# Retention in token-major form: all values and gates by seven products of halves, and the last dense layer's norm factor applied per token

## The chip, the cores and the metric

One core of a Trainium2 chip runs the whole program. The time is device microseconds from launch to end; lower is better. The kernel before was run three times: 1354.38, 1354.49 and 1355.02 us, median 1354.49. One further execution was recorded by the hardware profiler; its span is 1353.1 us.

Engines are called by the profile's names: PE is TensorE (PEld its weight loads), DVE VectorE, ACT ScalarE, POOL GpSimd, and SP the engine that issues most DMA transfers.

## What is computed

A trunk of two residual layers over 512 tokens of width 1024. Layer 0 mixes by a chunked spatial gating MLP, layer 1 by retention; each is followed by a dense MLP with a squared ReLU. Cut to what matters here:

```python
def retention(xn, w_in, head_norm_g, w_out):
    q, k, v, g = split(xn @ w_in)          # 4 heads: q, k of 256, v, g of 512
    q, k = rotary(q, cos, sin), rotary(k * dk ** -0.5, cos, sin)
    ...                                    # causal scores with decay; o = scores @ v
    o = rmsnorm(o, head_norm_g)            # per head
    return (o * silu(g)) @ w_out

def squared_relu_mlp(h, w1, w2):
    a = relu(h @ w1)
    return (a * a) @ w2

for i in range(2):
    x = x + mixer_i(rmsnorm(x, norm_mix_g[i]))
    x = x + squared_relu_mlp(rmsnorm(x, norm_ffn_g[i]), mlp_w1[i], mlp_w2[i])
return rmsnorm(x, final_norm_g)
```

## The kernel before

**Precision.** Every operand of a large matmul is split in two: a rounded high part (ACT copies, L234 for weights) and the difference (DVE subtracts, L241). A product is three matmuls: high x high, high x low, low x high (`mm3`, L277 to L281). A 128-wide piece over the whole width of 1024 is 24 matmuls.

**Tiling.** Tokens lie along the moving side in the feature-major stages: a tile holds 128 features by 512 tokens. The residual `xT` is kept so. In the token-major stages a tile holds 128 tokens by 512 features.

**Steps and pieces.** The program is a list of steps. Each takes weight pieces of 128 x 1024 numbers. After the matmuls of a step, `refill` puts in the splitting of the pieces to come: the high part three pieces ahead, the low part two ahead. Between steps hang hooks ("behind" a step), and `advance` moves unfinished chains of evacuations one stage on. So each engine's order is fixed in the code; what an engine reaches late delays all that stands behind it on that engine. Weights come in transfers of 1 MB into two buffers of their own (`raw`), and in some stretches also into spare large buffers (`more`).

**Seven products of halves.** `seven` (L480) computes a 1024 x 1024 block for 512 tokens as Strassen does: the tokens, the contraction and the output are each halved, and seven products of halves take the place of eight, 24 matmuls each, 168 instead of 192. Sums of weight halves are made by the DMA itself: an accumulating transfer, issued by POOL, adds one half onto another. Sums of activation halves ("sides": `sa`, `sd`, `sp`) are made by DVE and ACT and split in high and low. The products land in PSUM in token-major form and are added to the output tile by DVE; the first addition to a tile is a copy by ACT. Products are numbered 0 to 6; a `form` call makes the side of one of them.

**Retention before.** Values of heads 0 and 1 come by seven products (`smva`, `smvb`, `smvc`), interleaved with q/k pieces of head 0 and gate pieces of head 0. Values of heads 2 and 3 (`vv`) come by plain token-major products, all gates (`g`) by plain feature-major pieces. Attention (`av`, L1143) works on chunks of 128 features: for each of four key blocks it multiplies the values by the scores of all later tokens, so its matmuls are 512, 384, 256 and 128 columns wide. The norm of a head needs a sum over features, which lie along partitions: squares are summed by POOL, two matmuls with ones (`st_h`) add across partitions, and a third (`bc_h`) spreads the factor to all partitions. DVE multiplies it in and splits (`make_y`).

**The dense layers.** `dense` runs up pieces (feature-major) and seven products (token-major) in turn. In both layers an up piece is evacuated by DVE (ReLU and the norm factor, L953) and squared by ACT (L954).

## Time and profile before

| | |
|---|---|
| median of three runs | 1354.49 us |
| span of the profiled execution | 1353.1 us |
| DVE busy | 868.0 us |
| ACT busy | 581.0 us |
| mixer of layer 1 (retention) on PE | 619.0 to 1013.2 us |
| last dense layer on PE | 1013.2 to 1344.7 us |
| bytes moved by DMA | 182.43 MB |

How to read the rows: a timeline row gives the start in us from the span's start, the duration, the engine, the line, the operation, and output <- inputs by the program's names; "x4" merges four in a row, and brackets hold the idle time before it and what ended it. A group row ends with "| busy us, mean ns | idle before". A row of windows gives the stretch, its length, busy time (and count) of PE, PEld, DVE, ACT and POOL, the granted PE clock, the DMA share and GB/s.

### The profile page before, as it was taken

Reading aid. Unit: us, or ns where it says so; the run is one execution under the profiler, and the core shown is the slowest. Engines: PE = TensorE matmul, PEld = TensorE weight load, DVE = VectorE, ACT = ScalarE, POOL = GpSimd, SP = SyncE. Lnnn points to the kernel's source line nnn. Section 1 sums busy time; section 2 is a strip of 40 time slices with the busy share of each in tenths; the row PEclk is TensorE's granted clock in tenths of the full one; section 3 lists DMA queues with packets and bytes.
Section 4 is the critical chain, followed back from the end, with each engine's and each line's share of the span. In section 5 each row is a group of like instructions: output and inputs, shape, how many; then the busy total and the mean of one; then the engine's idle time right before and its main releaser. Section 6 shows DMA issues by size and latency. Waiting matters only on the chain.

```text
span 1353.1 us, 15298 instructions
## 1 busy us (share of the span) xinstructions
PE 1342.5 (99%) x6106; PEld 1117.2 (83%) x6106; DVE 868.0 (64%) x1101; ACT 581.0 (43%) x827; POOL 190.3 (14%) x145
## 2 busy tenths in 40 slices
PE   9999999999999999999999999999999999999997
PEld 7888888888888888888888888888888888888886
DVE  7754456665656656678946456557494675665697
ACT  5655443235544434524533343224333543443464
POOL 4100121130100000012201101111221000100003
PEclk9999999999999999999999999999999999999999
DMA  8662221245674747515712122221126375686763
GB/s 304 169 166 81 90 94 63 93 151 152 149 203 127 215 129 182 167 61 191 172 63 93 63 90 91 85 93 64 63 94 201 106 182 140 169 202 172 198 171 94
DMA packets 124439, 182.43 MB, mean 135 GB/s; under 512 B 3200, under 2 KB 68304, under 8 KB 124368
## 3 DMA queue, kind: packets, MB, share of 16 engines
q1 hardware_dynamic: 105040, 143.17, 31.2%
q0 software_dynamic: 19008, 37.75, 16.2%
q8 instruction: 48, 0.79, 0.2%
q10 hardware_dynamic: 320, 0.53, 0.1%
q14 instruction: 23, 0.19, 0.0%
HBM read 179.35 MB, written 2.10 MB: 134 GB/s over the span
## 4 chain that ended last, share of the span: by engine, by line
PE 97%; DVE 2%; ACT 1%; POOL 0%; issue 0%; ACTq 0%; POOLq 0%; DVEq 0%
PE up L281 24%; PE qk L281 6%; PE u L281 6%; PE o L281 6%; PE g L281 6%; PE ro L281 6%; PE dn L281 2%; PE vv L281 2%; PE av L281 2%; PE v L852 2%; PE smva L281 2%; PE smwa L281 2%; PE v L281 2%; PE sm12a L281 2%; PE sm11a L281 2%; PE sm10a L281 2%
## 5 line engine op out<-in xcount | busy, mean ns | idle before, releaser
L241 DVE TENSOR_TENSOR wL<-raw,wH 128x1024 fp32r<-128x1024 f32 x235 | 305.0, 1301 | 43.8 <-ACT wH L234 15.6
L234 ACT CAST wH<-raw 128x1024 fp32r<-128x1024 f32 x235 | 245.3, 1045 | 63.5 <-ACT wH L234 8.9
L281 PE MATMUL up<-hH,wH 128*128 128x512 f32 x480 | 187.2, 390 | 0.2 <-ACT xtok L1283 0.2
L281 PE MATMUL up<-hH,wL 128*128 128x512 f32 x480 | 186.8, 389 | 0.0
L281 PE MATMUL up<-hL,wH 128*128 128x512 f32 x480 | 186.8, 389 | 0.0
L953 DVE SCALAR_TENSOR_TENSOR r<-up,wide 128x512 f32<-128x512 f32 x54 | 37.4, 692 | 153.6 <-PE up L281 146.2
L954 ACT ACTIVATE aF<-r 128x512 f32<-128x512 f32 x54 | 34.2, 633 | 222.6 <-DVE r L953 222.6
L281 PEld LDWEIGHTS up<-hH,wH 128*128 128x128 f32 x480 | 90.1, 188 | 18.9 <-ACT xtok L1283 0.5
L281 PEld LDWEIGHTS up<-hH,wL 128*128 128x128 f32 x480 | 90.1, 188 | 18.9
L281 PEld LDWEIGHTS up<-hL,wH 128*128 128x128 f32 x480 | 90.1, 188 | 18.7
L207 POOL DMA_DIRECT2D raw<-in_mlp_w_dram x25 | 33.1, 1381 | 437.9 <-DVE wL L241 193.1
L310 POOL TENSOR_TENSOR ssq<-ssq,sq 128x512 f32<-128x512 f32 x28 | 44.1, 1577 | 117.0 <-ACT sq L309 116.7
L241 DVE TENSOR_TENSOR wL<-more,wH 128x1024 fp32r<-128x1024 f32 x42 | 51.0, 1217 | 4.5 <-issue 3.0
L234 ACT CAST wH<-more 128x1024 fp32r<-128x1024 f32 x42 | 44.0, 1047 | 15.9 <-ACT wH L234 6.0
L281 PE MATMUL o<-yH,wH 128*128 128x512 f32 x128 | 50.8, 396 | 0.0
L281 PE MATMUL g<-hH,wH 128*128 128x512 f32 x128 | 50.5, 394 | 0.0
L281 PE MATMUL u<-hH,wH 128*128 128x512 f32 x128 | 50.2, 393 | 0.0
L281 PE MATMUL qk<-hH,wH 128*128 128x512 f32 x128 | 50.0, 391 | 0.0
L281 PE MATMUL ro<-ryH,wH 128*128 128x512 f32 x128 | 49.9, 390 | 0.0
L281 PE MATMUL u<-hH,wL 128*128 128x512 f32 x128 | 49.9, 390 | 0.0
L281 PE MATMUL ro<-ryH,wL 128*128 128x512 f32 x128 | 49.9, 390 | 0.0
L281 PE MATMUL g<-hH,wL 128*128 128x512 f32 x128 | 49.9, 390 | 0.0
(450 smaller groups left out, 3050.1 us busy)
## 6 DMA issues: line engine op xcount, KB each, us to landing
raw<-in_mlp_w_dram SPq DMA_DIRECT2D x50, 1024.0 KB, 5.1
raw<-in_mlp_w_dram POOLq DMA_DIRECT2D x25, 1024.0 KB, 8.8
raw<-in_b_w_in_dram SPq DMA_DIRECT2D x22, 1024.0 KB, 5.0
more<-in_mlp_w_dram SPq DMA_DIRECT2D x21, 1024.0 KB, 5.3
raw<-in_a_w_in_dram SPq DMA_DIRECT2D x10, 1024.0 KB, 5.3
raw<-in_a_w_out_dram SPq DMA_DIRECT2D x8, 1024.0 KB, 4.9
raw<-in_b_w_out_dram SPq DMA_DIRECT2D x8, 1024.0 KB, 4.8
morew<-in_a_w_in_dram SPq DMA_DIRECT2D x5, 1024.0 KB, 8.5
```

What stands on the lines that cost most here:

```text
L207: nc.gpsimd.dma_start(out=r.tile, in_=src, accum_op=ALU.add)
L234: nc.scalar.copy(out=p.hi, in_=p.src)
L241: nc.vector.tensor_sub(out=p.lo, in0=p.src, in1=f32(p.hi))
L281: nc.tensor.matmul(ps, lhsT=a, rhs=b, start=start and i == 0, stop=stop and i == 2, skip_group_check=resumed)
L310: nc.gpsimd.tensor_tensor(out=state["ssq"], in0=state["ssq"], in1=sq, op=ALU.add)
L852: nc.tensor.matmul(accs0[n], lhsT=h[kk][:, n * P : (n + 1) * P], rhs=w, start=kk == 0 and j == 0, stop=kk == 7 and j == 2)
L953: nc.vector.scalar_tensor_tensor(out=r, in0=ps, scalar=0.0, in1=rbc, op0=ALU.max, op1=ALU.mult)
L954: nc.scalar.activation(a, r, AF.Square)
```

## The change

1. All values and all gates of retention come by seven products of halves: four runs of two heads each (`v` and `g` for heads 0 and 1, `w` and `j` for heads 2 and 3). The values run and the gates run of a pair share their sides (`kept`). For the second pair the sides are made from hF, the sum of the high and low parts of the normed input (`side_f`, `whole`), since the residual has been added to by then. The gates runs take the products in the order 1, 4, 0, 3, 5, 2, 6.
2. Attention and gating are token-major: `av` makes 128 tokens by 512 features at a time from the key blocks up to that token block. The head's norm is a sum along the free axis that ACT makes with the square; the gated output is multiplied by it per token and then transposed by PE (`turned`), which ACT and DVE evacuate as the high and low part.
3. The rotary tables take the place of the norm factor's tile, and decay tables are loaded head by head.
4. In the last dense layer the norm factor is left out of the up pieces. ReLU and square are both done by ACT; since the factor enters squared, its square (a power of -1 instead of -0.5) is applied per token where the products are added (`scaled`).

The core of the diff:

```diff
+    def norm_squares(name):
+        yield from stats(state["ssq"], r2s[:, 0, :], 1.0 / D, name, mone)
+        nc.vector.tensor_scalar(out=r2s[:, 1, :], in0=r2s[:, 0, :], scalar1=-1.0, scalar2=0.0, op0=ALU.mult, op1=ALU.add)
...
+        def add_to(m, n, t, op, bank):
+            m, n = 2 * m + t, 1 - n if swap else n
+            v, sign = dst[n][:, m, :], op == ALU.subtract
+            if (n, m // 2) in fresh:
+                nc.scalar.activation(v, bank, AF.Copy, scale=-1.0 if sign else 1.0)
+            elif scaled:
+                nc.vector.scalar_tensor_tensor(out=v, in0=bank, scalar=r2s[:, int(sign), m : m + 1], in1=v, op0=ALU.mult, op1=ALU.add)
+            else:
+                nc.vector.tensor_tensor(out=v, in0=v, in1=bank, op=op)
...
+            if l == 1:
+                nc.scalar.activation(a, ps, AF.Relu)
+                nc.scalar.activation(a, a, AF.Square)
+                return iter(())
...
+        def whole(b):
+            aF[8 + b] = hF[b] = big([P, 4, T], F32, f"hF{b}")
+            for i in range(4):
+                nc.vector.tensor_add(out=hF[b][:, i, :], in0=f32(hH[4 * b + i]), in1=f32(hL[4 * b + i]))
...
-    def av(h, c):
+    def av(h, n):
...
-        for j in range(NT):
-            s = slice(POFF[j], POFF[j] + T - j * P)
-            mm3(ps[:, j * P :], vhi[:, j, cs], vlo[:, j, cs], ph[:, s], pl[:, s], j == 0, j == NT - 1)
+        for j in range(n + 1):
+            s = slice(POFF[j] + (n - j) * P, POFF[j] + (n - j + 1) * P)
+            mm3(ps, ph[:, s], pl[:, s], vhi[:, j, :], vlo[:, j, :], j == 0, j == n)
...
+            y, ss, ms, r = gates(h)[:, n, :], ssh[:, h, n : n + 1], msh[:, h, n : n + 1], rh[:, h, n : n + 1]
+            nc.vector.tensor_tensor(out=y, in0=ps, in1=y, op=ALU.mult)
+            nc.scalar.activation(tmp(f"sqh{h}{n}", "sq"), ps, AF.Square, accum_out=ss)
+            yield
+            nc.vector.tensor_scalar(out=ms, in0=ss, scalar1=1.0 / DV, scalar2=EPS, op0=ALU.mult, op1=ALU.add)
+            rsqrt(r, ms, 1)
+            nc.scalar.activation(y, y, AF.Copy, scale=r)
...
+    def turned(h, c, bank=acc):
...
+            nc.tensor.transpose(ps[:, n * P : (n + 1) * P], gates(h)[:, n, c * P : (c + 1) * P], ident)
...
+        nc.scalar.activation(hi, ps, AF.Copy, scale=g)
+        nc.vector.scalar_tensor_tensor(out=lo, in0=ps, scalar=g, in1=f32(hi), op0=ALU.mult, op1=ALU.subtract)
...
+    hooksV[0].update({(0, 0): nxt(nrm1), (1, 0): norm_ready, (3, 0): lambda: form_v[0](5)})
+    take("vqqvqvqvvvv", v=prodV[0], q=qk_pieces(0, {0: nxt(nrm1, 2), 3: lambda: form_v[0](4)}))
...
+    take("gggqgqgqgqg", g=prodG[0], q=qk_pieces(1, {}, (acc, acc)))
...
+    hooksV[1].update({(0, 0): some(turned, 1, (0, 1)), (0, 1): some(turned, 1, (2, 3))})
+    take("vovovoovvvv", v=prodV[1], o=o_pieces(1))
...
+    take("gggqgqgqqgg", g=prodG[1], q=qk_pieces(3, {2: lambda: silu(2, range(4)), 3: some(av, 2, (0, 1))}, (acc, acc)))
+    do(lambda: (some(turned, 2, range(4))(), split_v(3, range(4)), silu(3, range(4))))
+    take("oooo", o=o_pieces(2, {0: some(av, 3, (0, 1)), 1: some(av, 3, (2, 3)), (3, 0): some(turned, 3, range(4))}))
+    take("oooo", o=o_pieces(3, {}, FFN + 8))
```

In the strings of `take`, v and g are products (two pieces, 24 matmuls), q is a q/k piece and o an output piece (24 matmuls each).

How the order of instructions moves is shown at three places. First DVE in the first values run, from the low part of product 3's last weights on. Names: wL is the low part of a weight piece, sav and spv the sums and the split side of the next product, m the rotary products of q/k, qkL their low part. In the kernel before, wL_4849 belongs to a gate piece and wL_4876 and wL_4905 to product 4:

```order
L241 TENSOR_TENSOR wL_4818<-raw_4105,wH_4817 128x1024
L1080 TENSOR_TENSOR m_4853<-qk_4741,tab 128x512
L1081 TENSOR_TENSOR m_4856<-qk_4741,tab 128x512
L1082 TENSOR_TENSOR m_4854<-qk_4823,tab 128x512
L1083 TENSOR_TENSOR m_4855<-qk_4823,tab 128x512
L241 TENSOR_TENSOR wL_4849<-raw_4684,wH_4848 128x1024
L618 SCALAR_TENSOR_TENSOR sav<-xT_87,gT,sav 128x256 x4
L648 TENSOR_TENSOR spv_4879<-sav,spv_4879 128x512 x2
L1092 TENSOR_TENSOR qkL_4688<-m_4853,qkH_4687 128x512
L1092 TENSOR_TENSOR qkL_4688<-m_4855,qkH_4687 128x512
L241 TENSOR_TENSOR wL_4876<-morev_4544,wH_4875 128x1024
L241 TENSOR_TENSOR wL_4905<-morev_4544,wH_4904 128x1024
```

In the changed kernel, after the same wL (wL_4821), the same engine has these; wL_4852 and wL_4891 are the two halves of product 4's weights:

```order
L638 SCALAR_TENSOR_TENSOR sav<-xT_92,gT,sav 128x256 x4
L668 TENSOR_TENSOR spv_4859<-sav,spv_4859 128x512 x2
L1155 TENSOR_TENSOR m_4868<-qk_4743,wide 128x512
L1156 TENSOR_TENSOR m_4871<-qk_4743,wide 128x512
L1157 TENSOR_TENSOR m_4869<-qk_4826,wide 128x512
L1158 TENSOR_TENSOR m_4870<-qk_4826,wide 128x512
L250 TENSOR_TENSOR wL_4852<-raw_4772,wH_4851 128x1024
L638 SCALAR_TENSOR_TENSOR sav<-xT_91,gT,sav 128x256 x4
L668 TENSOR_TENSOR spv_4894<-sav,spv_4894 128x512 x2
L1167 TENSOR_TENSOR qkL_4687<-m_4868,qkH_4686 128x512
L1167 TENSOR_TENSOR qkL_4687<-m_4870,qkH_4686 128x512
L250 TENSOR_TENSOR wL_4891<-raw_4772,wH_4890 128x1024
```

The gate piece's wL is gone, side 4 has moved ahead of the rotary products, and side 5 (the second sav and spv) now stands between the two halves of product 4's weights.

Second, DVE where a head's output is made ready for its output pieces. Before (head 1; gt is the gated output, ryL its low part, ro the output pieces' results), this lies among head 0's output pieces:

```order
L785 TENSOR_TENSOR xT_87<-xT_87,ro_20_6074 128x512
L241 TENSOR_TENSOR wL_6068<-raw_5967,wH_6067 128x1024
L1184 TENSOR_TENSOR gt_5411<-gt_5411,wide 128x512 x2
L1187 TENSOR_TENSOR ryL_6109<-gt_5411,ryH_6108 128x512 x2
L785 TENSOR_TENSOR xT_87<-xT_87,ro_21_6091 128x512
L785 TENSOR_TENSOR xT_87<-xT_87,ro_30_6117 128x512
L241 TENSOR_TENSOR wL_6105<-raw_5967,wH_6104 128x1024
```

In the changed kernel ryL comes from the transposes (yt) that PE makes between and behind the halves of product 0 of the second values run; hF is the recombined input, sax and spx the side of product 1, and wL_5998 the low part of the first output piece of head 1:

```order
L1103 TENSOR_TENSOR hF_6003<-hH_4415,hL_4416 128x512 x4
L805 TENSOR_TENSOR xT_92<-xT_92,ro_31_5981 128x512
L250 TENSOR_TENSOR wL_5998<-raw_5895,wH_5997 128x1024
L597 TENSOR_TENSOR sax_6028<-hF_5961,hF_6003 128x512
L597 TENSOR_TENSOR sax_6031<-hF_5961,hF_6003 128x512
L616 TENSOR_TENSOR spx_6027<-sax_6028,spx_6027 128x512
L616 TENSOR_TENSOR spx_6027<-sax_6031,spx_6027 128x512
L1236 SCALAR_TENSOR_TENSOR ryL_6037<-yt_6038,gT,ryH_6036 128x512
L1236 SCALAR_TENSOR_TENSOR ryL_6037<-yt_6045,gT,ryH_6036 128x512
L250 TENSOR_TENSOR wL_6024<-raw_5886,wH_6023 128x1024
L1236 SCALAR_TENSOR_TENSOR ryL_6037<-yt_6068,gT,ryH_6036 128x512
L1236 SCALAR_TENSOR_TENSOR ryL_6037<-yt_6075,gT,ryH_6036 128x512
```

The low parts of a head's output have moved from a piece and more ahead of their use to directly in front of it, behind the new side.

Third, PE in attention. Before, one chunk of 128 features:

```order
L281 MATMUL av_5395<-pH_5189,vvH_5201 128x512
L281 MATMUL av_5395<-pL_5190,vvH_5201 128x512
L281 MATMUL av_5395<-pH_5189,vvL_5202 128x512
L281 MATMUL av_5395<-pH_5189,vvH_5201 128x384
L281 MATMUL av_5395<-pL_5190,vvH_5201 128x384
L281 MATMUL av_5395<-pH_5189,vvL_5202 128x384
L281 MATMUL av_5395<-pH_5189,vvH_5201 128x256
L281 MATMUL av_5395<-pL_5190,vvH_5201 128x256
L281 MATMUL av_5395<-pH_5189,vvL_5202 128x256
L281 MATMUL av_5395<-pH_5189,vvH_5201 128x128
L281 MATMUL av_5395<-pL_5190,vvH_5201 128x128
L281 MATMUL av_5395<-pH_5189,vvL_5202 128x128
```

In the changed kernel, the first token block and the start of the second:

```order
L290 MATMUL av_5425<-vvH_5244,pH_5091 128x512
L290 MATMUL av_5425<-vvL_5245,pH_5091 128x512
L290 MATMUL av_5425<-vvH_5244,pL_5092 128x512
L290 MATMUL av_5435<-vvH_5244,pH_5091 128x512
L290 MATMUL av_5435<-vvL_5245,pH_5091 128x512
```

Values and scores have changed sides: all matmuls are 512 columns wide, and token block n has 3 (n + 1) of them.

More of the change, by code (lines that the diff above doesn't have):

```diff
@@ L38, in __init__ @@
         self.extra = True
+        self.after = 0
         if over is not None:
@@ L187, in load_raws @@
             r = raws[pos["raw"]]
+            if pos["done"] < r.after:
+                return
             if r.over is not None:
@@ L478, in trunk, with seven @@
     fresh = set()
-    def seven(w, row, col, a, dst, name, plan=range(7), behind={}, after={}, last=None, apart=False):
+    def seven(w, row, col, a, dst, name, plan=range(7), behind={}, after={}, last=None, apart=False, scaled=False, swap=False):
         def part(i, j):
-            r, c = row + 512 * i, col + 512 * j
+            r, c = row + 512 * i, col + 512 * (1 - j if swap else j)
             return w[r : r + 512, c : c + 512].rearrange("(k p) n -> p k n", p=P)
@@ L1041, in trunk @@
     QW, KW, VW, GWT = 0, H * DK, 2 * H * DK, 2 * H * DK + H * DV
[L1042 to L1056 removed]
+    POFF = [0, 512, 896, 1152]
@@ new lines, in trunk, with __init__, __missing__, kept @@
+    tab, qk, vv, pp = {}, {}, {}, {}
+    class Lazy(dict):
+        def __init__(self, name):
+            self.name = name
+        def __missing__(self, n):
+            self[n] = big([P, NT, DV], F32, f"{self.name}{n}")
+            return self[n]
+    vF, gF = [Lazy("vF0"), Lazy("vF2")], [Lazy("gF0"), Lazy("gF2")]
+    def kept(make):
+        made = {}
+        def a(s):
+            if s not in made:
+                made[s] = make(s)
+            return made[s]
+        return a
+    def side_f(name):
+        hF = {}
+        sums = side_acts(8, name)
+        def whole(b):
+            aF[8 + b] = hF[b] = big([P, 4, T], F32, f"hF{b}")
+            for i in range(4):
+                nc.vector.tensor_add(out=hF[b][:, i, :], in0=f32(hH[4 * b + i]), in1=f32(hL[4 * b + i]))
+        def make(s):
+            if s in (0, 2, 6):
+                k0, t0 = {0: (0, 0), 2: (4, 0), 6: (4, 2)}[s]
+                return lambda k, t: tuple(v[k0 + k][:, (t0 + t) * P : (t0 + t + 1) * P] for v in (hH, hL))
+            return sums(s)
+        return whole, make
@@ new lines, in twofold @@
+    def twofold(c, dst, side, name, plan, hooks, swap=False):
+        return seven(bw, 0, c, side, dst, name, plan, hooks, swap=swap)
+    PLAN_G = (1, 4, 0, 3, 5, 2, 6)
+    hooksV, hooksG = [{}, {}], [{}, {}]
+    whole, make_f = side_f("x")
+    sides = [kept(side_h(MIX + 8, "v")), kept(make_f)]
+    tV, form_v, prodV = zip(*[twofold(VW + 1024 * i, vF[i], sides[i], "vw"[i], range(7), hooksV[i]) for i in range(2)])
+    tG, form_g, prodG = zip(*[twofold(GWT + 1024 * i, gF[i], sides[i], "gj"[i], PLAN_G, hooksG[i], True) for i in range(2)])
@@ L1058, in load_decay, with values, gates @@
+    down_last(MIX + 8, {4: lambda: raws.append(tV[0])})
+    nrm1 = norm("mix1", True)
+    def values(h):
+        return vF[h // 2][h % 2]
+    def gates(h):
+        return gF[h // 2][h % 2]
     def load_decay(h):
-        nc.sync.dma_start(out=tab["t"][:, 2:4, :], in_=decay[:, h : h + 2, :])
-    def trig_scaled():
-        for i in range(2):
-            nc.vector.tensor_mul(tab["t"][:, i, :], tab["raw"][i], rbc)
+        tab[h] = tmp(f"dec{h}", "ssq", 1)
+        nc.sync.dma_start(out=tab[h], in_=decay[:, h, :])
@@ L1227, in both, with o_pieces, seq, some @@
+        nc.scalar.activation(hi, ps, AF.Copy, scale=g)
+        nc.vector.scalar_tensor_tensor(out=lo, in0=ps, scalar=g, in1=f32(hi), op0=ALU.mult, op1=ALU.subtract)
+    def o_pieces(h, behind={}, gcol=None):
+        pl = pieces_o(b_w_out[0], (h * DV, (h + 1) * DV), (0, D))
+        return [lambda i=i: out_piece(pl[i], i, h, "ro", gcol, between=behind.get((i, 0)), behind=behind.get(i)) for i in range(4)]
+    def seq(*fns):
         return lambda: [f() for f in fns]
-    def with_scores(h, of):
-        hn, sc = head_norm(of), each(scores, h)
-        fin = {0: nxt(hn), 1: nxt(hn, 2), 2: both(nxt(hn), lambda: make_y(of, (0, 1))), 3: lambda: make_y(of, (2, 3))}
-        return {i: both(sc[i], fin[i]) for i in range(4)}
+    def some(fn, h, ns):
+        return lambda: [(advance(), fn(h, n)) for n in ns]
@@ L1235, in begin_values, with anew @@
+    def anew():
+        fresh.update((n, m) for n in range(2) for m in range(2))
     def begin_values():
-        extra.extend(big([P, 2048], F32, f"morev{i}") for i in range(2))
-        fresh.update((n, m) for n in range(2) for m in range(2))
-        for n in range(2):
-            vF[n] = big([P, NT, DV], F32, f"vF{n}")
-        load_b()
-        form_v(0)
+        anew()
+        tab["raw"] = [zt(f"trg{i}") for i in range(2)]
+        for i in range(2):
+            nc.sync.dma_start(out=tab["raw"][i], in_=trig[:, i, :])
+        form_v[0](0)
@@ L1270, in trunk, with take @@
-    v_unit(3, with_scores(3, 2))
-    g_unit(3, each(av, 3))
-    o_unit(2, behind=finish_head(3))
-    o_unit(H - 1, gcol=FFN + 8)
+        load_decay(0)
+    def take(what, **of):
+        left = {k: list(v) for k, v in of.items()}
+        for w in what:
+            left[w].pop(0)()
+    hooksV[0].update({(0, 0): nxt(nrm1), (1, 0): norm_ready, (3, 0): lambda: form_v[0](5)})
+    do(begin_values)
+    take("vqqvqvqvvvv", v=prodV[0], q=qk_pieces(0, {0: nxt(nrm1, 2), 3: lambda: form_v[0](4)}))
@@ new lines, in trunk @@
+    take("qqqq", q=qk_pieces(2, {0: seq(some(turned, 0, (0, 1)), some(scores, 1, (0, 1))), 1: seq(some(turned, 0, (2, 3)), some(scores, 1, (2, 3))),
+                                 2: lambda: split_v(1, range(4)), 3: lambda: silu(1, range(4))}, (acc, acc)))
+    take("oooo", o=o_pieces(0, {0: some(av, 1, (0, 1)), 1: some(av, 1, (2,)), 2: seq(some(av, 1, (3,)), lambda: whole(0)), 3: lambda: whole(1)}))
+    raws.append(tV[1])
+    tV[1].after = len(order) - 2
+    do(lambda: (anew(), form_v[1](0)))
```

182 lines of the change are left out of this document (56 added, 126 removed).

## The prediction

> **What bounds the kernel now.** I read the page's busy shares first, then the chain of waits, then every wait of TensorE.
>
> ```profile
> span 1353.1 us, 15298 instructions
> PE 1342.5 (99%) x6106; PEld 1117.2 (83%) x6106; DVE 868.0 (64%) x1101; ACT 581.0 (43%) x827; POOL 190.3 (14%) x145
> PE 97%; DVE 2%; ACT 1%; POOL 0%; issue 0%; ACTq 0%; POOLq 0%; DVEq 0%
> PE warm L1395 <- POOL ident masks.py:199: 1.4, 1, 1.4
> PE av L281 <- DVE pL L1140: 0.3, 1, 0.3
> PE up L281 <- ACT xtok L1283: 0.2, 1, 0.2
> ```
>
> TensorE is busy 99% of the span, and all its waits are 1.4 us at the start plus 0.5 us. So the time is the sum of its instructions, a start of 1.4 us and a tail; the other engines count only where they make it wait. The median, 1354.49, stands 1.4 us above the profiled span. I carry that 1.4 over.
>
> A matmul's duration (0.39) is not its price, because matmuls overlap; the price is the distance from start to start:
>
> ```profile
> 642.01 0.39 PE L281 MATMUL qk<-hH,wH 128*128 128x512 f32 x1
> 652.89 0.39 PE L281 MATMUL qk<-hH,wH 128*128 128x512 f32 x1
> 732.98 0.39 PE L281 MATMUL av<-pH,vvH 128*128 128x512 f32 x1
> 734.84 0.44 PE L281 MATMUL g<-hH,wH 128*128 128x512 f32 x1
> 1029.53 1.03 PE L1282 MATMUL tt<-ident,xT 128*128 128x128 f32 x8
> 1030.32 0.48 PE L281 MATMUL up<-hH,wH 128*128 128x512 f32 x1
> 770.28 0.40 PE L355 MATMUL st_h<-st_h,onesr 128*128 128x512 f32 x1
> 770.75 0.40 PE L281 MATMUL vv<-wH,hH 128*128 128x512 f32 x1
> ```
>
> Between the first two rows stand 48 matmuls of 512 columns (a q/k piece and a product of 24 each): 10.88 / 48 = 0.2267 us. One feature chunk of attention, 12 matmuls of 512, 384, 256 and 128 columns, takes 1.86. Eight transposes take 0.79, 0.099 each. Two matmuls of a head's norm take 0.47, 0.235 each.
>
> **TensorE's sum.** Products: g was 384 matmuls and vv 192, 576 in all. They become three more runs of seven products of 24, 504. Minus 72 x 0.2267 = **-16.3**. Attention: 16 chunks x 1.86 = 29.8 become 4 heads x (1+2+3+4) blocks x 3 = 120 matmuls x 0.2267 = 27.2, so **-2.6**: the narrow matmuls cost more per column than the wide ones. Norms: 12 matmuls of the four heads and one of the last dense layer go, 13 x 0.235 = **-3.1**. The 64 new transposes cost 64 x 0.099 = **+6.3**. Sum **-15.7**. None of these can hide, on an engine that is 99% busy. Without new waits the time would be 1354.5 - 15.7 = 1338.8.
>
> **New waits: the first values run.** Before, a g piece of 24 matmuls (5.44 us) stood between products 3, 4, 5 and 6 and gave VectorE time. Now they follow each other. The rows of before at that place:
>
> ```profile
> 648.97 1.21 DVE L241 TENSOR_TENSOR wL<-raw,wH 128x1024 fp32r<-128x1024 f32 x1
> 654.21 1.28 DVE L529 TENSOR_TENSOR vF<-vF,smvb 128x512 f32<-128x512 f32 x2
> 655.40 1.22 DVE L241 TENSOR_TENSOR wL<-raw,wH 128x1024 fp32r<-128x1024 f32 x1
> 656.54 0.68 DVE L1080 TENSOR_TENSOR m<-qk,tab 128x512 f32<-128x512 f32 x1
> 658.53 0.69 DVE L1082 TENSOR_TENSOR m<-qk,tab 128x512 f32<-128x512 f32 x1 [0.71 <-PE qk L281]
> 659.74 2.00 DVE L241 TENSOR_TENSOR wL<-raw,wH 128x1024 fp32r<-128x1024 f32 x1
> 661.66 2.70 DVE L618 SCALAR_TENSOR_TENSOR sav<-xT,gT,sav 128x256 f32<-128x256 f32 x4
> 664.28 1.47 DVE L648 TENSOR_TENSOR spv<-sav,spv 128x512 fp32r<-128x512 f32 x2
> 665.67 1.28 DVE L1092 TENSOR_TENSOR qkL<-m,qkH 128x512 fp32r<-128x512 f32 x2
> 666.87 1.22 DVE L241 TENSOR_TENSOR wL<-morev,wH 128x1024 fp32r<-128x1024 f32 x1
> 672.24 0.89 DVE L618 SCALAR_TENSOR_TENSOR sav<-xT,gT,sav 128x256 f32<-128x256 f32 x2 [1.01 <-ACT sav L611]
> 674.23 0.89 DVE L618 SCALAR_TENSOR_TENSOR sav<-xT,gT,sav 128x256 f32<-128x256 f32 x2 [1.10 <-ACT sav L611]
> 675.03 1.48 DVE L648 TENSOR_TENSOR spv<-sav,spv 128x512 fp32r<-128x512 f32 x2
> 659.36 1.29 POOL L1084 TENSOR_TENSOR m<-m,m 128x512 f32<-128x512 f32 x1 [1.16 <-issue]
> 660.62 2.27 POOL L1085 TENSOR_TENSOR m<-m,m 128x512 f32<-128x512 f32 x1
> 663.77 0.39 PE L281 MATMUL g<-hH,wH 128*128 128x512 f32 x1
> ```
>
> Up to 656.54 VectorE's list is the same in both kernels, so I start there. Where g starts at 663.77, product 4 now starts. Its first half, 12 matmuls, lasts 2.72, so its second half is due at 666.5, and its second matmul needs that half's wL. VectorE has in front of it: side 4 (four sav at 0.4, as two take 0.89 at 672.24, and two spv in 1.39, from 664.28 to 665.67), 3.0, to 659.5; four m at 0.60 (two operations of that size from 654.21 to 655.40), to 661.9; the first half's wL, 1.92 beside POOL's rotation as at 659.74, to 663.9, just in time; side 5, which waits for ScalarE between its halves, 672.24 to 676.4, so 4.2, with 0.4 more for the rest of POOL's work, to 668.5; two qkL, 1.2 (665.67 to 666.87), to 669.7; the wL itself, 1.14 (655.40 to 656.54), to 670.9. TensorE waits from 666.7 to 670.9, about 4.2, to which I add 0.3 for hand-overs: **+4.5**. Bounds: 3 if POOL's work falls elsewhere, 5.5 if it overlaps in full. Behind this wait the products 5 and 6 need one wL each per 2.72, and VectorE recovers.
>
> On POOL's price the Trainium skill has a harder rule ("SBUF — State Buffer", Who interferes with whom): a VectorE instruction with two SBUF inputs and a GpSimd instruction that reads SBUF exclude each other, and the loser waits for the whole instruction. The trace agrees in part: the wL at 659.74 took 1.92 instead of 1.14 but began while POOL was running. By the rule this term would be 5.1, not 4.5.
>
> **The second values run.** Head 1's outputs are transposed behind product 0 (L1232), and the head's output piece follows at once, reading what VectorE makes of them (ryL, 4 x 512).
>
> ```profile
> L953 DVE SCALAR_TENSOR_TENSOR r<-up,wide 128x512 f32<-128x512 f32 x54 | 37.4, 692 | 153.6 <-PE up L281 146.2 <-ACT wide L373 7.4
> L956 ACT ACTIVATE aF<-up 128x512 f32<-128x512 f32 x6 | 3.6, 601 | 6.8 <-PE up L281 6.8
> L1119 DVE SCALAR_TENSOR_TENSOR vvL<-vv,r,vvH 128x512 fp32r<-128x512 f32 x8 | 5.4, 742 | 0.0
> 1067.00:1149.00 82.00, 82.00 (x364) 67.89 (x363) 53.11 (x67) 34.77 (x44) 5.20 (x4) 1.00 0.64 167
> ```
>
> From the end of attention's last block for head 1, VectorE's list up to the fourth ryL holds 16 operations of 512 columns (eight of them the new hF) at 0.60, three wL at 1.14, four ryL at 0.61 to 0.74 (vvL, also from PSUM) and one small: about 15.9, and 0.25 until the block's result is there. TensorE in that time does 24 + 24 matmuls and 16 transposes, 12.5, and 10 matmuls of the output piece, 2.27, before it needs the fourth ryL: 14.75. **+1.4** (0 to 2.5). Twelve matmuls of output piece 2 there take the PSUM bank that product 2's addition has just left: one addition behind one wL, **+0.5** (0 to 1). In front of head 2's output piece the same chain just fits: **+0.3** (0 to 1.5). Waits **+6.7** in all, bounds 3 to 10.5.
>
> **At nothing.** The last dense layer's evacuations go from VectorE (r, 0.69) to a second ScalarE instruction of 0.6 (L956), one per 10.9 us pair of pieces; the window of that layer shows ScalarE busy 34.8 of 82 us and VectorE 53.1, so both fit. If the cover were gone, each of the 27 would cost 0.6, 16 in all. Its 60 additions take the factor as a scalar per token, about 0.07 longer (vvL's 0.742 against r's 0.69 at most), 4 us in 330 on an engine with a third of its time free; only the last one, in the tail, counts. Score tables, trig tables and silu per token replace equal work.
>
> **Forecast.** 1354.5 - 15.7 + 6.7 = **1345.5** (1342 to 1346.8), chance 0.45.
>
> **Rivals.** (1) VectorE keeps up: its wL stand two pieces ahead of their use, and if sides 4 and 5 were done earlier than my list says, waits stay at 0 to 3 us: 1338.8 to 1341.8. Against it speaks that VectorE in the rows above has one gap between 654 and 668, the 0.71 at 658.53, and side 4 now fills it. Chance 0.22.
>
> (2) The clock drops in the long gap.
>
> ```profile
> 1344.30 0.39 PE L281 MATMUL sm13a<-wH,sp 128*128 128x512 f32 x1
> 1345.00:1353.00 8.00, 0.00 (x0) 0.00 (x0) 2.53 (x5) 2.78 (x6) 2.21 (x3) 0.73 0.35 131
> 4.08 1.11 PE L680 MATMUL xt<-ident,xr 128*128 128x128 f32 x4
> 7.63 0.60 PE L680 MATMUL xt<-ident,xr 128*128 128x128 f32 x4
> ```
>
> The last matmul ends at 1344.7. A mean clock of 0.73 over the 8 us from 1345 is full speed for 3.7 us and half for the rest, so it halves 4.0 us after TensorE stopped. My gap is 4.5. At the start, the four transposes at 4.08 took 1.11 and those at 7.63 took 0.60, and the first matmul ran at 1.4: TensorE needs 2.7 to 6.2 us of work to get its clock back, and loses half of that, 1.3 to 3.1. Time 1346.8 to 1348.6. Chance 0.25. The Trainium skill ("TensorE: Matmul & The Clock Gate", What's actually happening) says that one idle window of about 3.4 us halves the clock, that the window runs freely and that a busy one restores it; by it a gap of 4.5 holds a whole window about once in three times. The trace's 4.0 fits.
>
> (3) More places like the first: the second values run also has products 3 to 6 in a row. Its sides are cheaper (no scaling; two sums and two differences, 2.4 at 0.60) and its spare is about 1 us per product. If each of the four products and the gates' runs lost 1 to 2 us: 1350 to 1357, within 0.2% or near. Chance 0.05.
>
> (4) Slower: the accumulating loads come late.
>
> ```profile
> raw<-in_b_w_in_dram POOLq DMA_DIRECT2D x3, 1024.0 KB, 8.4
> raw<-in_b_w_in_dram SPq DMA_DIRECT2D x22, 1024.0 KB, 5.0
> ```
>
> Twelve such loads are added (16 instead of 4), now with two plain weight buffers instead of four. A plain and an accumulating load take 13.4 us; in the first values run product 5's buffer is free at 650.1 (after the wL at 648.97) and its use is due at 663.77 + 5.44 = 669.2, 19 us later, and I read the other runs as no tighter. So it decides where the two loads take over 17 (two for the splitting); at 19 each of the twelve would cost 2, 24 in all, 1370. Against it: in the dense layer's window above, with such loads and a DMA share of 0.64, TensorE was busy 82.00 of 82.00 us. Chance 0.03.
>
> **Chances.** Faster by over 0.2% (2.7 us, about what a measurement of this kernel tells from no change): 0.92, from the forecast and the first two rivals; same 0.05; slower 0.03. The range, 1338.5 to 1349, takes in the bounds of the waits and both nearer rivals.
>
> **What would show it.** TensorE's instructions 5942 in the program instead of 6035, its start-to-start distance still 0.2267, its busy time down by about 15 us; a wait of 4 to 5 us on a wL (L250) in smvc, about 666 us from the start; one of 1 to 2 us on ryL (L1236) in front of ro near 810. Wrong if the attention blocks take more than 0.2267 per matmul, if the transposes take more than 0.1, or if wH in ScalarE waits for DMA.

## The result, and the profile after

The changed kernel takes **1360.18 us** (median of six, 1357.54 to 1361.90), the kernel before 1354.45. The ratio is 1.0040, 95% interval 1.0030 to 1.0051: slower by 0.4%, where 1345.5 was forecast, faster by 0.7%. The profiled execution is the slowest of the six, 1361.9, with a span of 1359.9.

From the page of the changed kernel, the span and the busy shares:

```profile
span 1359.9 us, 15249 instructions
PE 1332.7 (98%) x6013; PEld 1103.3 (81%) x6013; DVE 867.5 (64%) x1092; ACT 635.8 (47%) x918; POOL 196.0 (14%) x154
```

TensorE has the 93 matmuls fewer that the change takes away (6106 to 6013) and the span is 6.8 us longer. What was taken away was priced rightly. From the chain of work that ended last, in order of time, with start, length and count:

```profile
748.39 2.72 PE smga L290 x12
751.11 2.04 PE av L290 x9
753.15 2.72 PE smga L290 x12
755.87 2.72 PE av L290 x12
```

and two timeline rows around the new transposes:

```profile
817.10 1.03 PE L1232 MATMUL yt<-ident,gF 128*128 128x128 f32 x8
817.89 0.48 PE L290 MATMUL smwa<-wH,hH 128*128 128x512 f32 x1
```

A product's half is 12 matmuls in 2.72, attention 9 in 2.04, both 0.227 each, and eight transposes take 0.79 (817.10 to 817.89), all as forecast. By these prices 15.7 us did leave TensorE's sum. The waits of TensorE tell what came back (engine, tile, what it waited for: us in total, times, longest):

```profile
PE smvc L290 <- DVE wL L250: 4.5, 1, 4.5
PE qk L290 <- DVE wL L250: 2.5, 2, 1.5
PE ro L290 <- ACT ryH L1235: 2.1, 1, 2.1
PE ro L290 <- DVE vF L528: 1.6, 1, 1.6
...
PE av L290 <- ACT sqh L1218: 1.4, 1, 1.4
PE smjc L290 <- ACT wH L243: 1.3, 1, 1.3
PE ro L290 <- DVE ryL L1236: 1.2, 3, 0.6
PE smjc L290 <- DVE wL L250: 0.8, 1, 0.8
PE smwa L290 <- DVE vF L528: 0.5, 1, 0.5
```

These nine rows are 15.9 us in 12 waits; the kernel before had 0.5 beside the start, and the forecast added 6.7. And the clock that TensorE was granted dropped to half twice in the middle of the program. In the table by stretches the columns are busy time of TensorE, its weight loads, VectorE, ScalarE and POOL, then the granted clock, DMA share and GB/s:

```profile
668.70:672.11 3.41, 0.69 (x3) 0.59 (x4) 3.41 (x5) 3.41 (x7) 0.00 (x0) 1.00 1.14 207
672.11:675.52 3.41, 3.41 (x10) 2.66 (x9) 2.12 (x3) 1.03 (x2) 0.00 (x0) 0.50 1.08 292
880.33:883.74 3.41, 1.45 (x5) 0.99 (x6) 2.22 (x2) 3.30 (x4) 0.00 (x0) 1.00 0.00 0
883.74:887.15 3.41, 3.41 (x10) 2.63 (x9) 1.65 (x3) 1.56 (x4) 1.28 (x1) 0.50 0.28 31
```

Each half-clock stretch is 3.41 us long and loses half of it, 1.7: 3.4 in all.

The forecast named as a sign of being wrong that ScalarE's high parts (wH) wait for transfers. They do. From the page:

```profile
L243 ACT CAST wH<-raw 128x1024 fp32r<-128x1024 f32 x259 | 269.4, 1045 | 128.0 <-DMA raw<-in_b_w_in_dram 26.8
```

Of ScalarE's idle time before these copies, 26.8 us ended with a transfer of retention's input weights; in the same stages of the kernel before it was 1.6. Only a little of it costs directly: TensorE waited for such a wH 1.3 us.

### The profile page after: what moved, and what is told of

The parts are those of the page before. It is cut to its first block, busy times and chain, and to the rows that moved or that the text cites. A ratio compares the mean times of both kernels' runs of the same rounds, so it can differ in the third digit from the quotient of the medians.

```text
span 1359.9 us, 15249 instructions
## 1 busy us (share of the span) xinstructions
PE 1332.7 (98%) x6013; PEld 1103.3 (81%) x6013; DVE 867.5 (64%) x1092; ACT 635.8 (47%) x918; POOL 196.0 (14%) x154
## 4 chain that ended last, share of the span: by engine, by line
PE 86%; DVE 6%; DMA 3%; ACT 2%; POOL 1%; issue 1%; ACTq 0%; POOLq 0%; DVEq 0%; SPq 0%
PE up L290 24%; PE u L290 6%; PE o L290 6%; PE ro L290 6%; PE qk L290 4%; DMA raw<-in_b_w_in_dram 3%; PE dn L290 2%; DVE wL L250 2%; PE v L872 2%; PE smwa L290 2%; PE v L290 2%; PE sm12a L290 2%; PE sm11a L290 2%; PE sm10a L290 2%; PE sm02a L290 2%; PE sm01a L290 2%
## 5 line engine op out<-in xcount | busy, mean ns | idle before, releaser
L250 DVE TENSOR_TENSOR wL<-raw,wH 128x1024 fp32r<-128x1024 f32 x259 | 332.2, 1289 | 124.4 <-issue 42.2
L243 ACT CAST wH<-raw 128x1024 fp32r<-128x1024 f32 x259 | 269.4, 1045 | 128.0 <-DMA raw<-in_b_w_in_dram 26.8
L984 ACT ACTIVATE aF<-r 128x512 f32<-128x512 f32 x27 | 17.1, 633 | 115.6 <-DVE r L983 115.6
L983 DVE SCALAR_TENSOR_TENSOR r<-up,wide 128x512 f32<-128x512 f32 x27 | 18.7, 692 | 81.2 <-PE up L290 78.1
L972 ACT ACTIVATE aF<-up 128x512 f32<-128x512 f32 x30 | 18.0, 601 | 90.1 <-PE up L290 90.1
L290 PE MATMUL qk<-hH,wL 128*128 128x512 f32 x128 | 50.1, 392 | 2.5 <-DVE wL L250 2.5
L290 PE MATMUL ro<-ryL,wH 128*128 128x512 f32 x128 | 50.1, 391 | 0.9 <-DVE ryL L1236 0.9
L616 DVE TENSOR_TENSOR sp<-aF,sp 128x512 fp32r<-128x512 f32 x42 | 27.1, 687 | 36.1 <-ACT sp L613 36.1
```

What stands on the lines that cost most here:

```text
L243: nc.scalar.copy(out=p.hi, in_=p.src)
L250: nc.vector.tensor_sub(out=p.lo, in0=p.src, in1=f32(p.hi))
L290: nc.tensor.matmul(ps, lhsT=a, rhs=b, start=start and i == 0, stop=stop and i == 2, skip_group_check=resumed)
L616: nc.vector.tensor_sub(out=lo, in0=vs[c], in1=f32(hi))
L972: nc.scalar.activation(a, ps, AF.Relu)
L983: nc.vector.scalar_tensor_tensor(out=r, in0=ps, scalar=0.0, in1=rbc, op0=ALU.max, op1=ALU.mult)
```

## The experiments

The time of a kernel with such waits scatters by some us: 1357.54 to 1361.90 here, 1354.34 to 1355.19 before. Half clocks that come or not are a part of it, but not all: the run with the lowest mean clock, 0.994, took 1360.55, the slowest had 0.996. So each run is read by its waits and by the clock in its profile, and the span of that one profiled execution stands beside the median. The changed kernel has 1359.9 and 1360.18, but its span is that of its slowest execution (the six go from 1355.5 to 1359.9). A difference of spans against it therefore comes out too large, and the medians show less: 1.9 for e1, 0.9 for e4, 1.7 for e9, 0.6 for e14.

**Rotary one step later (e1).**

```diff
-        if h == 0:
+        if h != 2:
             yield
```

> The rotary's second stage (high copy by ScalarE, low difference by VectorE) comes one step later for heads 1 and 3, as it does for head 0 in both kernels. Theory (order): since a gates product is two steps of 2.72 us where a gate piece was one of 5.44, the low difference is issued while POOL still works on the rotation, and VectorE stands still for it 1.5 us with the weights' low parts behind it; so the waits of TensorE on wL in qk (1.00 and 1.52 us) and on sqh in av (1.41) go, 4 us and 0.1 to 0.2 of refilling each: 1355.7 from 1360.2. Rival (late weights: the accumulating loads fill the DMA queues): the wL waits stay, since their wH are cast after transfers that landed late, and only the one in av goes: 1358.7.

Median 1358.28 (1356.63 to 1363.09), span 1355.8, 4.1 shorter. The rows of qk and of av are gone from the waits; the others stand. The median lies nearer the rival's 1358.7, but the wL waits, which the rival kept, are gone. In the changed kernel VectorE, POOL and ScalarE (timeline) show why:

```profile
923.12 0.68 DVE L1158 TENSOR_TENSOR m<-qk,wide 128x512 f32<-128x512 f32 x1
923.35 1.29 POOL L1159 TENSOR_TENSOR m<-m,m 128x512 f32<-128x512 f32 x1 [14.29 <-DVE m L1157]
924.67 0.62 ACT L1166 CAST qkH<-m 128x512 fp32r<-128x512 f32 x1 [2.15 <-POOL m L1159]
925.33 1.94 DVE L1167 TENSOR_TENSOR qkL<-m,qkH 128x512 fp32r<-128x512 f32 x2 [1.53 <-ACT qkH L1166]
927.19 2.35 DVE L250 TENSOR_TENSOR wL<-raw,wH 128x1024 fp32r<-128x1024 f32 x2
```

On VectorE the low difference stands straight behind the m, a step of 2.72 us later, while POOL is still at the rotation and ScalarE's high copy waits for POOL. VectorE stands 1.53 us, and the wL behind it comes late. In e1 a wL stands between them. These are three places in the gates runs, none of them in my forecast.

**Orders of the values runs (e2, e3).**

```diff
-    hooksV[0].update({(0, 0): nxt(nrm1), (1, 0): norm_ready, (3, 0): lambda: form_v[0](5)})
+    hooksV[0].update({(0, 0): nxt(nrm1), (1, 0): norm_ready})
...
-    take("vqqvqvqvvvv", ... {0: nxt(nrm1, 2), 3: lambda: form_v[0](4)}))
+    take("vqqvvqvqvvv", ... {0: nxt(nrm1, 2), 3: lambda: form_v[0](5)}))
```

> The first values run takes its pieces in the order v0 q0 q1 v1 v2 q2 v3 q3 v4 v5 v6, so that q pieces stand ahead of product 3 and of product 4, with product 5's side formed behind q3. Theory (order): VectorE has more work than time between products 3 and 5; with the q pieces there the wait of 4.51 us on product 4's wL falls to 0 to 1.5, and the half clock behind it (3.41 us of records at 0.5, 1.7 us lost) goes too: 1354 to 1355.5 from 1360.2. Rival (late weights): three accumulating loads overlap there, the waits move to the weights of products 2 and 3, which now come a piece earlier: 1359 to 1362.

```diff
-    take("vovovoovvvv", v=prodV[1], o=o_pieces(1))
+    take("vovovovvovv", v=prodV[1], o=o_pieces(1))
```

> The second values run takes v o v o v o v v o v v instead of v o v o v o o v v v v. Theory (transfers): four products in a row and the gates' first product behind them ask for more than the queues bring (DMA share 1.06 from 860 to 870 us), and the gates' first weights land at 880.4 where TensorE wants them at 879.5; an output piece later among the products gives the loads 5.4 us, so the waits at 874 (0.52) and 880 to 883 (2.0) and the half clock at 883.7 (1.7 lost) go: 1356 from 1360.2. Rival (order of the engines' queues alone): the loads start when buffers come free and not by the order of the pieces; the waits stay: 1360.

Both forecasts were wrong, and both times are worse than their rivals': 1372.45 and 1372.61. ScalarE and POOL in e3:

```profile
876.05 1.04 ACT L243 CAST wH<-raw 128x1024 fp32r<-128x1024 f32 x1 [16.73 <-DMA raw<-in_b_w_in_dram]
864.96 2.59 POOL L216 DMA_DIRECT2D raw<-in_b_w_in_dram  x2 [34.85 <-DMA raw<-in_b_w_in_dram]
867.89 1.28 POOL L216 DMA_DIRECT2D raw<-in_b_w_in_dram  x1 [0.33 <-issue]
```

Product 5's weights need a buffer, a plain load, an accumulating load on top, and the split. The buffer comes free only when product 4's weights are split, so three accumulating loads go out within 3 us, and ScalarE, which takes its work in order, stands 16.7 us at the cast, with the next side's copies behind it; TensorE waited 8.2 us. e2 is the same with 12.9 at ScalarE, and TensorE waited 6.6 and 6.2. What such loads cost in the changed kernel, by stretches:

```profile
658.00:674.00 16.00, 11.44 (x45) 8.72 (x44) 14.71 (x20) 9.29 (x16) 5.51 (x4) 0.94 1.11 200
674.00:676.00 2.00, 2.00 (x7) 1.60 (x6) 0.39 (x2) 0.11 (x1) 0.00 (x0) 0.62 1.04 391
```

In the first row three accumulating loads stand one behind the other, in the second plain ones: 200 GB/s against 391, with a DMA share of 1.11 and 1.04 (full). So a megabyte (1.05 million bytes) summed costs 5 us of all queues, a plain one 2.7.

**Head 2's transposes ahead of the scores (e4).**

```diff
-        (6, 0): some(scores, 3, (0, 1)), (6, 1): some(scores, 3, (2, 3)),
+        (6, 0): some(scores, 3, (0, 1)), (6, 1): seq(some(turned, 2, range(4)), some(scores, 3, (2, 3))),
...
-    do(lambda: (some(turned, 2, range(4))(), split_v(3, range(4)), silu(3, range(4))))
+    do(lambda: (split_v(3, range(4)), silu(3, range(4))))
```

> Head 2's outputs are transposed ahead of the last two blocks of head 3's scores instead of behind them. Theory (order): ScalarE copies two finished gates tiles (1.08 us) ahead of ryH and VectorE splits scores ahead of ryL; with the transposes first the wait of 2.14 us on ryH and the 0.29 on ryL go, and at most 0.7 comes back where the transposes wait for the norm: 1357.9 to 1358.5 from 1360.2. Rival: the chain from the last attention block to the gated output (two stages, POOL's power among them) ends too late, and the same 2 us are waited for at the transposes: 1360.

1359.32, span 1356.8. By the span it is 3.1 shorter, by the median 0.9, which misses the theory's 1.7 to 2.3. The waits show the mechanism: those on ryH (2.14) and on head 2's ryL (0.29) are gone, and nothing came back at the transposes. They were a place in ScalarE's and VectorE's order. In the changed kernel ScalarE has, as expected:

```profile
964.62 1.08 ACT L524 ACTIVATE gF<-smja 128x512 f32<-128x512 f32 x2
965.58 2.42 ACT L1235 ACTIVATE ryH<-yt,gT 128x512 fp32r<-128x512 f32 x4
```

**Head 0's key rotary later (e5).**

```diff
+        for _ in range(6 if (h, which) == (0, 1) else 0):
+            yield
         m = [zt(f"m{h}{which}{i}") for i in range(4)]
```

> Head 0's key rotary (four m of VectorE, two operations of POOL, two copies, two low differences) starts six steps later, behind product 5 instead of ahead of product 4. Theory (VectorE is full between products 3 and 5): 3.6 us of VectorE's work and POOL's overlap leave the stretch ahead of product 4's second wL, the wait of 4.51 us falls to 0 to 0.7 and the half clock behind it does not come: 1354 to 1355 from 1360.2. Rival (transfers, as in the reordered first values run, where the wH of product 5 waited 12.9 us for its load): three accumulating loads of 1 MB stand one behind the other from 656 us, and products 5 and 6 wait for them 2 to 4 us: 1357 to 1359.

1361.73. The wait at product 4 went, and one of the same length came at product 6. VectorE and TensorE in e5:

```profile
673.12 1.23 DVE L250 TENSOR_TENSOR wL<-raw,wH 128x1024 fp32r<-128x1024 f32 x1 [2.21 <-ACT wH L243]
674.26 0.68 DVE L1157 TENSOR_TENSOR m<-qk,wide 128x512 f32<-128x512 f32 x1
...
676.66 1.97 DVE L250 TENSOR_TENSOR wL<-raw,wH 128x1024 fp32r<-128x1024 f32 x1
678.54 1.27 DVE L528 TENSOR_TENSOR vF<-vF,smva 128x512 f32<-128x512 f32 x2
679.37 0.47 PE L290 MATMUL smva<-wH,hH 128*128 128x512 f32 x1 [4.51 <-DVE vF L528]
```

Product 6 sums on in the PSUM bank of product 5, so it waits for product 5's additions (vF), which I had put behind the moved m. VectorE's load was the cause at product 4. At product 6 the place that I chose was wrong, and the rival has a part too: VectorE stood 2.21 us for a wH whose weights landed late (ScalarE waited 3.59 for the transfer).

**Output pieces earlier (e6).**

```diff
-                if i == 0 and then is not None:
+                if i == 0 and then is not None and (name, s) != ("w", 2):
...
-    take("vovovoovvvv", v=prodV[1], o=o_pieces(1))
+    take("voovoovvvvv", v=prodV[1], o=o_pieces(1, {3: lambda: form_v[1](3)}))
```

> The second values run takes v o o v o o v v v v v, and product 3's side is formed behind the fourth output piece instead of behind product 2's first half. Theory (transfers and their room): the gates' first plain load takes the room of head 1's ryL, which the last output piece reads; that piece now ends 5.4 us earlier, so the load and the accumulating one behind it land before their use. The waits of 0.52 (874), 2.0 (880 to 883) and the half clock (1.7) go, and so does the 1.56 at 845, since no output piece takes product 2's bank any more: 1354 to 1355 from 1360.2. Rival: with five products in a row the queues are short for longer; weights or sides of products 3 to 6 are waited for by 4 us or more: 1360 or later.

The waits fell: 1.56 at 845 gone (1.02 came at the start of product 2, behind side 3), 2.0 at 880 down to 0.3; the one at 874 stayed. But the median is 1360.14: the profile has half clocks at 669 (6.83 us, two windows), 925 and 966, where the changed kernel has two of 3.41. The mechanism held in the main, the forecast of the time didn't.

**No sums of weights (e7)**, the accumulating loads of the second pair left out (so the kernel leaves out the sums of weight halves, and its values and gates of heads 2 and 3 aren't retention's):

```diff
-        t1 = Raw(part(0, 0), adds=[part(0, 1)])
+        def add(i, j):
+            return [part(i, j)] if sums else []
+        t1 = Raw(part(0, 0), adds=add(0, 1))
...
+        return seven(bw, 0, c, side, dst, name, plan, hooks, swap=swap, sums=name not in "wj")
```

> The eight accumulating loads of the second values run and the second gates run are left out, so their weight halves are not summed. Theory (transfers): weights land in time; the waits at 874 and 880 to 883 and the half clock go (4.2 us), the 1.56 at 845 shrinks to under 0.5, since the output weights cast at 839.8 come earlier; the waits on wL in qk (1.0, 1.5) and on sqh (1.4) stay: 1354.5 to 1356 from 1360.2. Rival (only the order on the engines' queues counts): the waits stay within 0.5 us: 1359.5 to 1360.5.

1356.63, span 1356.2. The waits at 874 and at 880 to 883 and the half clock there are gone, the 1.56 at 845 is 0.89; the waits on sqh, ryH and at 667 stand. So the second pair's waits on weights belong to the transfers. Of the two on wL in qk the later one (1.52, at 927) is gone here as it is in e1: it needs both, weights that land just in time and the rotary ahead of them.

**Filler in the gap (e8, e14).** Matmuls of the identity ahead of product 4's second half, 36 in e8 and 19 in e14:

```diff
                 bk = BANK[s]
+                if (name, s, i) == ("v", 4, 1):
+                    warm_up(36)
```

> 36 small matmuls of the identity (about 3.9 us at full clock) are added between the halves of product 4 of the first values run, where TensorE waits 4.51 us. Theory (clock): the time behind that wait at 0.5 (3.41 us in the records, 1.7 lost) belongs to TensorE standing still; with the filler the clock stays at 1.0 there and the span falls by 1.7, to 1358.5 median. Rival: the clock drops by its own, or the filler pushes the product back: no change or up to 0.5 longer.

> The changed kernel with 19 small matmuls (38 instructions; e8's 72 took 8.2 us, so 4.3) between the halves of product 4 of the first values run, where TensorE stands for 4.51. Theory (clock): no window of the record there has over 1 us without matmuls, the half clock at 671 to 675 does not come and 1.7 us are saved: 1358.5 from 1360.2, unless another place takes a half clock by its phase, which the record shows. Rival (the lost time behind the wait is the refilling of the pipeline and not the clock): 1360.2.

e8's filler overran the gap (72 instructions, 8.2 us), so the time, 1364.17, tells little. e14's fits it, 4.41 us for 38 instructions; of the wait 0.26 is left:

```profile
666.86 4.41 PE L1425 MATMUL warm<-ident 128*128 128x128 f32 x38
672.11:675.52 3.41, 3.41 (x16) 2.80 (x15) 3.39 (x5) 2.26 (x3) 0.00 (x0) 1.00 1.10 256
```

The same stretch that ran at 0.50 in the changed kernel (10 matmuls) has 1.00 (16 matmuls). The span is 1358.2, 1.7 shorter, the median 1359.62. By the clock in the profiles it was the standing still: behind this wait of 4.5 us a half clock stands in all seven profiles that have it (the changed kernel, e1, e3, e4, e6, e7 and e9), and in e8 and e14 there is none. The time alone does not settle it: the median is 0.6 shorter, and forecast was 1.7.

**Gates from product 0 (e9).**

```diff
-    PLAN_G = (1, 4, 0, 3, 5, 2, 6)
+    PLAN_G = (0, 1, 4, 3, 5, 2, 6)
...
+        (4, 1): some(scores, 0, (0, 1)), (3, 0): some(scores, 0, (2, 3)),
+        (3, 1): lambda: split_v(0, range(4)),
```

> Both gates runs take product 0 (plain weights, no side) ahead of product 1 (summed weights): 0 1 4 3 5 2 6 instead of 1 4 0 3 5 2 6; the scores of heads 0 and 2 move to behind product 4 and into product 3. Theory (transfers): the summed weights of product 1 land at 880.4, 0.9 us late with the half clock behind them; with 5.4 us more they are in time, and the waits of 2.0 us at 880 to 883 and 1.7 of half clock go: 1356.5 from 1360.2. Rival: product 0's own plain load stands behind the summed one in the list of loads and lands no earlier; the wait stays at 1 to 3 us: 1359 to 1361.

1358.50, span 1355.0, 4.9 shorter; the median, 1.7 shorter, lies between theory and rival. There is no wait at 874 or 880 and no half clock there, so by the waits the theory holds. In the changed kernel ScalarE shows the late weights:

```profile
880.44 2.94 ACT L243 CAST wH<-raw 128x1024 fp32r<-128x1024 f32 x3 [8.07 <-DMA raw<-in_b_w_in_dram]
```

**All together (e10, e12, e13).** e10 takes e1, e4, e6 (side 3 behind the third output piece), e9, the key rotary seven steps later, and:

```diff
-    raws.append(tG[0])
+    raws.insert(next(i for i, r in enumerate(raws) if r.over is tV[0]) + 1, tG[0])
...
-    take("oooo", o=o_pieces(0, {0: some(av, 1, (0, 1)), 1: some(av, 1, (2,)), 2: seq(some(av, 1, (3,)), lambda: whole(0)), 3: lambda: whole(1)}))
+    take("oooo", o=o_pieces(0, {0: seq(some(av, 1, (0, 1)), lambda: whole(0)), 1: seq(some(av, 1, (2,)), lambda: whole(1)), 2: some(av, 1, (3,))}))
```

> All changes of order together: rotary's second stage later (heads 1 and 3), head 0's key rotary seven steps later, the first gates run's summed weights loaded before the last loads of the first values run, head 2's transposes ahead of the scores, hF two pieces earlier, the second values run as v o o v o o v v v v v with side 3 behind the third output piece, and the gates' products from 0. Theory (the 22 us above TensorE's sum of 1338.8 are waits and half clocks of these places alone): waits of 2 to 4 us left, no half clock: 1340 to 1344, which beats the kernel before (1354.5). Rival (the rooms for weights are too few: each wait that goes lets the next transfer be late): 1348 to 1354.

> As e10, but with the gates' products in the order of the changed kernel (1 4 0 3 5 2 6). Theory (transfers at the second gates run are a place of their own): 2 to 4 us more than e10, since its product 1 waits for summed weights again: 1343 to 1347. Rival: earlier output pieces alone bring those weights in time: the same as e10 within 1 us.

e10 takes 1350.80, its rival's range; e12 (as e10, old order of the gates) 1352.39. Both beat the kernel before (ratios 0.9970, 0.9961 to 0.9979, and 0.9978, 0.9969 to 0.9987), neither reached what was expected. In e12:

```profile
PE smva L290 <- DVE vF L528: 2.0, 1, 2.0
PE smwa L290 <- DVE vF L528: 1.7, 1, 1.7
PE ro L290 <- DVE ryL L1238: 1.6, 2, 1.1
PE yt L1234 <- ACT gF L1224: 1.4, 1, 1.4
```

The first two are again additions that stand behind the split of weights that have not landed (VectorE: 1.40 idle for wH, two wL, then vF). The last two I put down to hF, moved ahead of head 1's norm; in e13, with half of it moved back, they are gone but for 0.3. In neither does TensorE wait for the second gates run's first weights, so there the rival of e12 holds: the earlier output pieces suffice. So e13 goes on from e12, with whole(0) behind output piece 0, whole(1) behind 3, and:

```diff
+                adds = i == 1 and s == 5 and name in "vw"
+                if adds:
+                    (m, n), op = OUT[s][0]
+                    for t in range(2):
+                        add_to(m, n, t, op, banks[BANK[s]][t])
...
                 refill()
...
+    hooksV[1].update({(0, 0): some(turned, 1, (0, 1)), (0, 1): some(turned, 1, (2, 3)), (3, 1): lambda: form_v[1](5)})
```

> As e12, and: product 5's additions of both values runs stand ahead of the splitting of the coming weights on VectorE, side 5 of the second values run is formed behind product 3 instead of inside product 4, and only the first half of hF is moved earlier. Theory (order): of e12's 8.1 us of waits the 2.0 at 675 and 1.7 at 871 are additions that stand behind the low parts of weights not yet landed, the 1.1 at 864 is the side behind such a wL, and 1.45 of head 1's transposes comes from hF ahead of the norm; these go to about 2 in all: 1346 from e12's 1352.4, with no half clock in the profile. Rival (transfers): the weights of products 5 and 6 themselves are late, TensorE then waits for wH or wL at the same places: 1350 to 1352.

**1347.81** (1346.01 to 1351.34), ratio to the kernel before 0.9951 (0.9937 to 0.9965). Its waits:

```profile
PE smva L290 <- ACT wH L243: 2.4, 1, 2.4
...
PE smwa L290 <- DVE wL L250: 0.8, 1, 0.8
PE smjc L290 <- DVE wL L250: 0.8, 1, 0.8
PE smjc L290 <- ACT wH L243: 0.4, 1, 0.4
```

The additions hold TensorE for no more than 0.3; what is left is mostly weights: 2.4 us for product 6's wH, the last of two accumulating loads. Theory and rival each had a part. One half clock follows that wait, at 678, against the expectation.

**The last dense layer alone (e11)**, part 4 put into the kernel before:

```diff
+            if l == 1:
+                nc.scalar.activation(a, ps, AF.Relu)
+                nc.scalar.activation(a, a, AF.Square)
+                return iter(())
```

> The kernel before with part 4 alone: ReLU and square of the last dense layer on ScalarE, its factor in the additions, token-major. Theory of the prediction: hidden but for one norm matmul less and 0.1 in the tail: 1354.4, within 0.3 of before. Rival (from the profile of the changed kernel, whose tail behind the last matmul is 1.1 us longer): the longer additions push the last norm's first half past its place, +0.8: 1355.3. A second ScalarE instruction that stood on the path would give +16: 1370.

1355.53 against 1354.85, ratio 1.0004 (0.9995 to 1.0014): the median has the rival's side, the interval holds both. The profile is plainer: from the last matmul's start to the end 9.6 us instead of 8.8, the layer itself 0.2 shorter. The 16 us that a second ScalarE instruction on the path would have cost are not there.

## Why the prediction was wrong

The forecast had the kernel faster with chance 0.92 and slower with 0.03; it is slower. What left TensorE was right, what came back was not.

- **TensorE's sum, -15.7: right.** Matmul pitch, attention and transposes came as priced. e13 agrees: its span of 1345.9 less 4.9 of new waits, 1.7 of half clock and about 1.2 of refilling (below) is 1338.1; the span before, 1353.1, less 15.7 and with 1.0 of longer tail is 1338.4. TensorE's busy time fell by 9.8 and not 15 because matmuls at half clock and behind a wait count longer (in e12, without a half clock, it fell by 13.8).
- **First values run, +4.5: right in place and size** (4.51 at 666.9, on wL, VectorE behind by side 5 and the rotary). What the term left out is what follows: the forecast had the clock as a rival against it, and both came.
- **POOL's price in it was low.** VectorE and POOL in the changed kernel:

```profile
661.85 2.00 DVE L250 TENSOR_TENSOR wL<-raw,wH 128x1024 fp32r<-128x1024 f32 x1
663.77 1.90 DVE L638 SCALAR_TENSOR_TENSOR sav<-xT,gT,sav 128x256 f32<-128x256 f32 x2
661.47 1.28 POOL L1159 TENSOR_TENSOR m<-m,m 128x512 f32<-128x512 f32 x1 [1.47 <-issue]
662.73 2.25 POOL L1160 TENSOR_TENSOR m<-m,m 128x512 f32<-128x512 f32 x1
```

  The wL ends 1.1 after POOL's first operation, the two sav 0.7 after its second, nearly as if each had waited for it in full (alone a wL takes 1.22 and two sav 0.88): 1.0 is added to the sav where I took 0.4. That agrees with the rule of the Trainium skill ("SBUF — State Buffer", Who interferes with whom: one excludes the other). By it the wait was to be 5.1; VectorE ended later by 0.4, but TensorE too came 0.2 later and the hand-over was short, hence 4.51.
- **ryL of head 1, +1.4: right in place**, 0.9 measured (of the 1.2; the rest is head 2). **Bank after product 2, +0.5: measured 1.6**, since the output weights landed late too (e7: 0.89). **Head 2, +0.3: measured 2.4**; I had not put ScalarE's copies of finished gates ahead of ryH.
- **The step that failed is the list itself**: the waits "+6.7 in all, bounds 3 to 10.5" come from four places, and of the loads it says "I read the other runs as no tighter". 15.9 us were measured. Three of the missing places have one thing in common that I did not work out: a gates product is two steps where a gate piece was one, so the rotary's second stage is issued in half the time (3.9 us, gone in e1; one of the three, 1.5, needs late weights too, e7). The others are the second gates run's weights and the additions in front of them (2.5 us, gone in e7 and e9).
- **Rival 3** (more places like the first, 1350 to 1357, chance 0.05) came nearest: the waits did lie in the second values run and the gates runs, mostly 0.5 to 2 us each. But the cause was the rotary and the weights, not the sides that it names, and the time is over its range.
- **Rival 4** (accumulating loads late) had a part of the mechanism and the wrong price: I gave each late load 2 us and the case 0.03. In fact few are late, but they can go out three at a time at 200 GB/s. The load for product 6, which the rival did not weigh, is late too, behind the longer wait on VectorE: with that wait gone, TensorE waits 2.0 (e12) and 2.4 (e13) for what this load holds up.
- **Rival 2** (clock): 1.7 per half-clock stretch, within the 1.3 to 3.1. It was priced for one gap of over 4.0 us; a gap of 2 us sufficed (at 880), and there were two such stretches. Nor does the gap of 4.5 lead to a half clock once in three times: it did in each of the seven profiles that have it.
- **At nothing:** the evacuations of the last dense layer were hidden. The tail was 1.1 us longer, not 0.1 (e11: 0.8). VectorE starts the first of the last two additions 0.81 after the last matmul's start (1350.80), where it started together with it before (1344.28). What stands ahead of it is a sum of squares that ScalarE ends later by as much. The longer additions would explain that, but it was not followed further.

Together, against the profiled execution (1361.9 to 1345.5, 16.4 over): waits 9.2 more than forecast, half clocks 3.4, tail 1.0, time outside the span 0.6 (2.0 instead of 1.4); the 2.2 left is about 0.18 for each of 12 waits, which I take for refilling (an estimate; directly seen is 0.11 of it: the first matmul behind a wait stands 0.34 from its successor instead of 0.23).

Open: whether a third buffer for weights would end the last 2.4 us of e13. It was not tried.

## What to carry to other kernels

Where an order written by hand counts stages in steps, a change that makes the steps shorter makes every staged chain earlier: look at each chain that waits for another engine. On an engine that is 99% busy, a saving is worth only what the other engines and the transfers can follow. So list every tile that the engine now needs in quick succession, with its buffer, load and split, and not the places that come to mind. Put what frees a bank or a tile ahead of work whose input may be late.
